# Attention in pairs of groups: one compressed softmax for eight heads, all transposes of a unit ahead of its value products

## The chip, the cores and the metric

The kernel runs on one core of a Trainium2 chip. What counts is the device time of one execution in microseconds (us); a kernel's time is the median of several executions. A core has TensorE (matrix products and transposes, results in PSUM banks), VectorE, ScalarE, GpSimd and SyncE, which issues transfers. Each engine runs its own instructions in a fixed order and waits on semaphores of the others.

## What is computed

Two decoder layers over 256 tokens of width 1024 in float32: gated linear attention first, native sparse attention (NSA) second. Only the second layer's attention is touched. It has 16 heads of width 64 in 4 groups of 4, and three branches. With 256 tokens, four blocks of 64 and sixteen selectable blocks every block is selected, so the selected branch is causal attention over all keys; the window of 512 covers all keys as well. The compressed branch attends to 15 blocks, of which a token sees those that have ended, and gives zero where there is none.

```python
s = jnp.einsum('bghtd,bgcd->bghtc', qb, kcmp)
valid = cmp_end[None, :] <= t[:, None]
pc = jax.nn.softmax(jnp.where(valid, s, NEG), axis=-1)
pc = jnp.where(jnp.any(valid, axis=-1)[:, None], pc, 0.0)
o_c = jnp.einsum('bghtc,bgcd->bghtd', pc, vcmp)
...
o_s = jnp.einsum('bghtks,bgtksd->bghtd', ps, v_sel)
...
o_w = jnp.einsum('bghts,bgsd->bghtd', jax.nn.softmax(s, axis=-1), vwin)
...
o = jnp.einsum('bshc,bshcd->bshd', gates, out).reshape(B, S, NSA_Q) * jax.nn.silu(z)
return o @ w_out.astype(jnp.float32)
```

## The kernel before

The tokens lie in two tiles of 128 (t = 0, 1). A *unit* is one group of four heads on one tile, `Unit(g, t)`: eight units. Products that need float32 accuracy are split into a high and a low part, so that one product becomes three (L211, L212, L213: high by high, high or low by the other); a weight is split by ScalarE (`hi`, L190) and by VectorE or GpSimd (`lo`, L196) from one of four buffers `raw` that transfers fill.

`scores()` of a unit runs per head: products of q with the high and low part of k (L1001; for t = 0 256 keys and 16 compressed ones in one bank, for t = 1 272 columns in one bank and 256 of the window branch in another that two heads share), VectorE's mask with the row's extreme (L1006), ScalarE's exponential with its sum (L1008), VectorE's addition of the compressed scores' mask into `cS` (L1027), and per two heads the coefficients gate/sum (L1039, L1041) by which GpSimd scales the probabilities P in place (L1045). After the fourth head `compressed()` (L1054 to L1060, with ScalarE's exponential L1056 between) makes the compressed probabilities of the four heads, 128 x 64.

`values()` of a unit has 2(t + 1) rounds, one for each branch and 128 keys. T of a round is four transposes of P into one bank (L1074) and a copy to pT, on ScalarE (L1078) and on VectorE (L1080) in turn; V of a round is two products of 64 columns of v with pT (L1088) that accumulate in half of the bank `o`, which the units use in turn. T runs two rounds ahead of V: T0, T1, V0, T2, V1, T3 and so on. In the last rounds but one stands Tc, the transpose of the compressed probabilities (L1094) with ScalarE's copy pcT (L1096), and the end is Vc, two products of pcT with the compressed values (L1112). `finish()` multiplies by the gate z and splits the result into `ofT` (L356 VectorE, L357 ScalarE, L358 VectorE).

Around them: `z_steps` (two projections for the gate, L211 to L213 of 256 columns, evacuated by L362), the loads and splits of the out-projection's weights, and `out_steps(t)`, 48 products of 512 columns per tile (L211 to L213 into two banks `acc`), of which an L213 is the first to need the low part of ofT. After the products of a bank the residual: L269 ScalarE, L271/L274/L276/L281 VectorE, L275 GpSimd, then the store.

The program text gives the units one after the other: units (0,0) and (1,0), z's first half, (2,0), z's second half, (3,0), `out_steps(0)`, then the four units of t = 1, and `out_steps(1)`. A scheduler of the framework sets the order of each engine's instructions from there, as its own estimate of the times decides; `after(ins, prev)` adds an edge that only fixes an order on the engine, `chain` ties the projections' products one behind the other, and one edge puts out_steps(1)'s products from k = 5 (`LATE`) behind the last product of unit (3,1). Banks of PSUM: acc 2, s (scores) 3, t (transposes) 2, o 1. Buffers: eight for P, three for pT.

Of the kernel before, what the change touches and what calls it, by code (L numbers as in the profile page):

```python
# [16 lines left out]
P = 128  # L17
# [70 lines left out]
def hybrid_kernel(ctx: ExitStack, tc: tile.TileContext, x, positions, pre_norm, post_norm,  # L88
# [893 lines left out]
    obank, on = bank("o"), [0]  # L982

    class Unit:


        def __init__(self, g, t):
            self.g, self.t, self.n = g, t, (t + 1) * P
            self.Pt = []

        def scores(self):
            g, t, n = self.g, self.t, self.n
            self.mn, self.sm, self.cS, self.cf = small(8, "mn"), small(8, "sm"), small(64, "cS"), small(8, "cf")
# [3 lines left out]
            c3 = self.cS.rearrange("p (h c) -> p h c", c=16)  # L997
# [12 lines left out]
            for i in range(4):  # L1010
# [244 lines left out]
```

## Time and profile before

| | us |
|---|---|
| three executions | 307.05, 307.33, 304.06; median 307.05 |
| the profiled execution | 302.72 |
| its span, first to last instruction | 300.8 |
| busy: TensorE / VectorE / ScalarE / GpSimd | 286.6 / 215.3 / 181.5 / 167.0 |
| mean granted TensorE clock | 0.984 of full speed |

Times within the span count from its first instruction; around it lie 1.9 us. The second layer's attention works from about 195 us to the end. A product's length in a timeline contains its filling of the pipeline, so that products that stand 0.23 us apart may each be 0.4 long: what a sequence costs is read from start to start. A line whose count is over one is several instructions in a row.

### The profile page before, as it was taken

Reading aid. Unit: us, or ns where it says so; the run is one execution under the profiler, and the core shown is the slowest. Engines: PE = TensorE matmul, PEld = TensorE weight load, DVE = VectorE, ACT = ScalarE, POOL = GpSimd, SP = SyncE. Lnnn points to the kernel's source line nnn. Section 1 sums busy time; section 2 is a strip of 40 time slices with the busy share of each in tenths; the row PEclk is TensorE's granted clock in tenths of the full one; section 3 lists DMA queues with packets and bytes.
Section 4 is the critical chain, followed back from the end, with each engine's and each line's share of the span. In section 5 each row is a group of like instructions: output and inputs, shape, how many; then the busy total and the mean of one; then the engine's idle time right before and its main releaser. Section 6 shows DMA issues by size and latency. Waiting matters only on the chain.

```text
span 300.8 us, 5374 instructions
## 1 busy us (share of the span) xinstructions
PE 286.6 (95%) x1788; PEld 239.7 (80%) x1788; DVE 215.3 (72%) x556; ACT 181.5 (60%) x468; POOL 167.0 (56%) x184
## 2 busy tenths in 40 slices
PE   7999999999999999889979999999997999999991
PEld 7888999999998887668958676899994678676660
DVE  1779569846979877576893536799999858877423
ACT  4896788667754757435534405679967637657301
POOL 1496968984383252927545035897799434172200
PEclk9999999999999999999999999999997799999998
DMA  7997588105677334394745785576144000100001
GB/s 214 403 362 217 151 258 288 56 22 186 204 220 212 92 82 130 64 289 147 195 162 144 274 263 180 190 218 232 42 142 139 2 0 0 71 2 0 2 0 71
DMA packets 28301, 44.57 MB, mean 148 GB/s; under 512 B 2865, under 2 KB 12513, under 8 KB 28274
## 3 DMA queue, kind: packets, MB, share of 16 engines
q1 hardware_dynamic: 28242, 44.23, 46.6%
q8 instruction: 14, 0.23, 0.3%
q14 instruction: 13, 0.11, 0.1%
q10 hardware_dynamic: 32, 0.01, 0.0%
HBM read 43.18 MB, written 1.05 MB: 147 GB/s over the span
## 4 chain that ended last, share of the span: by engine, by line
PE 63%; DVE 13%; issue 9%; POOL 6%; ACT 4%; DMA 3%; SPq 0%; POOLq 0%; DVEq 0%; ACTq 0%
PE acc L211 11%; PE acc L213 11%; PE acc L212 11%; PE s L468 4%; POOL lo L196 3%; PE s L212 3%; PE s L211 3%; PE s L213 3%; DVE lo L196 3%; PE o L894 3%; PE t L1074 3%; PE o L1088 3%; PE s L1001 2%; ACT hi L190 2%; DMA raw<-in_gla_w_in_dram 1%
## 5 line engine op out<-in xcount | busy, mean ns | idle before, releaser
L196 POOL TENSOR_TENSOR lo<-raw,hi 128x512 fp32r<-128x512 f32 (+2 forms) x63 | 82.8, 1334 | 44.4 <-ACT hi L190 44.4
L190 ACT ACTIVATE hi<-raw 128x512 fp32r<-128x512 f32 (+2 forms) x120 | 64.2, 583 | 37.7 <-DMA raw<-in_nsa_w_in_dram 26.6
L196 DVE TENSOR_TENSOR lo<-raw,hi 128x512 fp32r<-128x512 f32 (+2 forms) x57 | 53.6, 963 | 13.4 <-ACT hi L190 13.3
L1045 POOL TENSOR_SCALAR P<-P,cf 128x128 f32<-128x128 f32 (+1 forms) x64 | 29.2, 475 | 30.2 <-DVE cf L1041 14.4
L211 PE MATMUL acc<-hT,hi 128*128 128x256 f32 x160 | 45.2, 283 | 0.1
L212 PE MATMUL acc<-hT,hi 128*128 128x256 f32 x160 | 44.8, 280 | 0.0
L213 PE MATMUL acc<-hT,lo 128*128 128x256 f32 x160 | 44.5, 281 | 0.0
L211 PE MATMUL acc<-hi,hT 128*128 128x512 f32 (+2 forms) x112 | 39.2, 350 | 1.2 <-DVE yg L276 0.8
L213 PE MATMUL acc<-hi,hT 128*128 128x512 f32 (+2 forms) x112 | 38.9, 347 | 0.0
L212 PE MATMUL acc<-lo,hT 128*128 128x512 f32 (+2 forms) x112 | 38.8, 346 | 0.0
L1008 ACT ACTIVATE P<-P,mn 128x128 f32<-128x128 f32 (+1 forms) x64 | 28.4, 445 | 7.2 <-DVE mn L1006 5.9
L211 PEld LDWEIGHTS acc<-hT,hi 128*128 128x128 f32 x160 | 30.1, 188 | 0.4 <-DVE zT L362 0.3
L212 PEld LDWEIGHTS acc<-hT,hi 128*128 128x128 f32 x160 | 30.1, 188 | 0.1
L213 PEld LDWEIGHTS acc<-hT,lo 128*128 128x128 f32 x160 | 29.8, 188 | 0.0
L211 PEld LDWEIGHTS acc<-hi,hT 128*128 128x128 f32 x112 | 21.1, 188 | 5.3 <-ACT yg L269 1.2
L1006 DVE CUSTOM_DVE_ANT_0 P<-s,c 128x128 f32<-128x128 f32 (+1 forms) x64 | 20.6, 347 | 5.3 <-PE s L1001 4.4
L213 PEld LDWEIGHTS acc<-hi,hT 128*128 128x128 f32 x112 | 21.1, 188 | 2.9 <-DVE hT L311 0.4
L212 PEld LDWEIGHTS acc<-lo,hT 128*128 128x128 f32 x112 | 21.1, 188 | 2.0
L1074 PE MATMUL t<-c,P 128*128 128x128 f32 x96 | 17.4, 296 | 2.0 <-ACT pcT L1096 1.9
L440 POOL TENSOR_TENSOR lo<-raw,hi 128x512 fp32r<-128x512 f32 (+1 forms) x9 | 12.3, 1388 | 9.9 <-ACT hi L436 9.8
L1074 PEld LDWEIGHTS t<-c,P 128*128 128x128 f32 x96 | 11.1, 147 | 7.3 <-issue 3.6
L832 POOL TENSOR_TENSOR dup<-rt,rt 128x512 f32<-128x512 f32 x6 | 8.9, 1487 | 11.2 <-DVE rt L825 5.7
(268 smaller groups left out, 676.2 us busy)
## 6 DMA issues: line engine op xcount, KB each, us to landing
raw<-in_nsa_w_in_dram SPq DMA_DIRECT2D x24, 512.0 KB, 4.5
raw<-in_gla_w_in_dram SPq DMA_DIRECT2D x12, 512.0 KB, 6.1
raw<-in_gla_w_out_dram SPq DMA_DIRECT2D x8, 512.0 KB, 4.3
raw<-in_nsa_w_out_dram SPq DMA_DIRECT2D x8, 512.0 KB, 4.2
raw<-in_nsa_w_in_dram SPq DMA_DIRECT2D x8, 280.0 KB, 8.4
raw<-in_gla_w_in_dram SPq DMA_DIRECT2D x6, 344.0 KB, 3.4
home<-in_gla_w_in_dram SPq DMA_DIRECT2D x4, 512.0 KB, 6.7
w<-in_nsa_ck_w_dram SPq DMA_DIRECT2D x4, 512.0 KB, 3.8
```

The costliest lines, as they stand in the source:

```text
L190: m = after(nc.scalar.activation(hi[:, j, :n], raw[:, j, :n], AF.Copy), prev)
L196: eng.tensor_sub(lo[:, j, :n], raw[:, j, :n], f(hi[:, j, :n]))
L211: m = nc.tensor.matmul(o, a[0], b[0], start=start, stop=False, **kw)
L212: nc.tensor.matmul(o, a[0], b[1], start=False, stop=False, **kw)
L213: return m, nc.tensor.matmul(o, a[1], b[0], start=False, stop=stop, **kw)
L440: line(e, eng.tensor_sub(lo[:, j, :n], raw[:, j, :n], f(hi[:, j, :n])))
L468: m = nc.tensor.matmul(o[t][:, :chunk.n], hT[i][:, k, t * P:(t + 1) * P], w[j], start=(k == b == 0), stop=(k == KT - 1 and b == 2))
L894: nc.tensor.matmul(hid_b[kv * 64:(kv + 1) * 64, :CHID], flat[:, j, kv].rearrange("p g c -> p (g c)"), w1[u * 2 + kv][:, j % 4, :], start=( ...
L1006: nc.vector.tensor_tensor_reduce(out=o, in0=src, in1=masks[br], op0=ALU.add, op1=ALU.min, scale=-0.125, scalar=3.0e38, accum_out=self.mn[: ...
L1008: nc.scalar.activation(o, o, AF.Exp, scale=-1.0, bias=self.mn[:, j:j + 1], accum_out=self.sm[:, j:j + 1])
L1045: nc.gpsimd.tensor_scalar(o, o, cf[:, i * 2 + br:i * 2 + br + 1], 1.0, op0=ALU.mult, op1=ALU.mult)
L1074: pe(nc.tensor.transpose(b[:, i * P:(i + 1) * P], self.Pt[i][:, c0:c0 + P], ident))
```

## The change

A class `Pair` holds what two groups of a tile share: `cS` for eight heads (128 x 128), one compressed softmax for them (L1001 to L1007 in the changed file; the same seven operations as before, with 8 instead of 4 columns of sums), one bank with both transposes Tc (L1012) and one copy pcT (L1014), and Vc for either half (L1022). `scores()` is no generator any more; its lines are L1046 (products), L1051 (mask), L1053 (exponential), L1072 (cS), L1083/L1085 (coefficients) and L1089 (GpSimd). The text order is: scores of both groups, then values of both. `values()` issues all T of the unit (L1101; copies L1105 on ScalarE, L1108 on VectorE, the latter into two buffers of another pool, so that the three of pT are ScalarE's alone), in a pair's first unit then Tc, then all V (L1119), tied in their order and behind the last Vc before them, then Vc. The first V of a unit stands behind its last T or, in a pair's first unit, behind Tc. `out_steps(1)` gets two more edges: products from k = 1 behind T of the last unit's second round, from k = 2 behind T of its fourth. The bank `o` is shared as before; it is cleared only by the first product of a pair.

```diff
-    obank, on = bank("o"), [0]
+    obank, lastC = bank("o"), [None]
+
+    class Pair:
...
+        def begin(self):
+            self.cS = small(128, "cS")
+
+        def compressed(self):
+
+            p, t = self.p, self.t
+            gv = gates[:, t, 8 * p:8 * p + 8, :]
+            cS = self.cS
+            c3 = cS.rearrange("p (h c) -> p h c", c=16)
+            cm, cs = small(8, "cm"), small(8, "cs")
+            nc.vector.tensor_reduce(cm, c3, axis=AX.X, op=ALU.max)
+            nc.vector.tensor_tensor(c3, c3, cm.unsqueeze(2).to_broadcast([P, 8, 16]), op=ALU.subtract)
+            nc.scalar.activation(cS, cS, AF.Exp, scale=0.125)
+            nc.vector.tensor_reduce(cs, c3, axis=AX.X, op=ALU.add)
+            nc.vector.reciprocal(cs, cs)
+            nc.vector.scalar_tensor_tensor(cs, cs, cc("anyv")[:, t:t + 1], gv[:, :, 0], op0=ALU.mult, op1=ALU.mult)
+            nc.vector.tensor_tensor(c3, c3, cs.unsqueeze(2).to_broadcast([P, 8, 16]), op=ALU.mult)
+
+        def transpose(self):
+            b = bank()
+            for G in range(2):
+                self.Tc = nc.tensor.transpose(b[:64, G * P:(G + 1) * P], self.cS[:, G * 64:(G + 1) * 64], ident)
+            pcT = ap_.tile([64, 2 * P], F32, tag="pcT", name=nm("pcT"), bufs=1)
+            nc.scalar.activation(pcT, b[:64, :2 * P], AF.Copy)
+            self.pcT = pcT
+
+        def share(self, G, m):
+
+            ob = obank[:, G * 256:(G + 1) * 256]
+            for i in range(2):
+                w = vblk[:, 2 * self.p + G, 2 * i:2 * i + 2, :].rearrange("p a d -> p (a d)")
+                m = after(nc.tensor.matmul(ob[:, i * P:(i + 1) * P], w, self.pcT[:, G * P:(G + 1) * P], start=False,
+                                           stop=(i == 1), skip_group_check=True), m)
+            return m
 
...
         def scores(self):
             g, t, n = self.g, self.t, self.n
-            self.mn, self.sm, self.cS, self.cf = small(8, "mn"), small(8, "sm"), small(64, "cS"), small(8, "cf")
+            self.mn, self.sm, self.cf = small(8, "mn"), small(8, "sm"), small(8, "cf")
+            if g % 2 == 0:
+                self.pair.begin()
+            c3 = self.pair.cS[:, g % 2 * 64:(g % 2 + 1) * 64].rearrange("p (h c) -> p h c", c=16)
...
-                if i == 3:
-                    self.compressed()
-                yield 1
+            if g % 2:
+                self.pair.compressed()
...
         def values(self):
+
...
+            ob = obank[:, g % 2 * 256:(g % 2 + 1) * 256]
             rounds = [(br, y) for br in range(2) for y in range(t + 1)]
-            pTs = {}
...
+            pTs, self.T = [], []
+            for br, y in rounds:
                 b = bank()
                 c0 = br * n + y * P
                 for i in range(4):
-                    pe(nc.tensor.transpose(b[:, i * P:(i + 1) * P], self.Pt[i][:, c0:c0 + P], ident))
-                pT = ap_.tile([P, 512], F32, tag="pT", name=nm("pT"), bufs=N_PT)
+                    m = nc.tensor.transpose(b[:, i * P:(i + 1) * P], self.Pt[i][:, c0:c0 + P], ident)
                 evac[0] += 1
                 if evac[0] % 2:
+                    pT = ap_.tile([P, 512], F32, tag="pT", name=nm("pT"), bufs=N_PT)
                     nc.scalar.activation(pT, b, AF.Copy)
                 else:
+                    pT = lp.tile([P, 512], F32, tag="rt1", name=nm("pT"), bufs=2)
                     nc.vector.tensor_copy(pT, b)
-                pTs[r] = pT
-
...
+                pTs.append(pT)
+                self.T.append(m)
+            if g % 2 == 0:
+                self.pair.transpose()
+                m = self.pair.Tc
+
+            for r, (br, y) in enumerate(rounds):
                 kt = (t - y) if br == 0 else y
                 pv = pTs[r].rearrange("p (i a n) -> p a i n", i=2, a=2)
                 for a in range(2):
-                    pe(nc.tensor.matmul(ob[a * 64:(a + 1) * 64, :],
-                                        (vs_sb, vw_sb)[br][:, kt, g * DH:(g + 1) * DH], pv[:, a],
-                                        start=(br == y == 0), stop=False, skip_group_check=True))
-
...
+                    v = nc.tensor.matmul(ob[a * 64:(a + 1) * 64, :], (vs_sb, vw_sb)[br][:, kt, g * DH:(g + 1) * DH],
+                                         pv[:, a], start=(r == 0 and g % 2 == 0), stop=False, skip_group_check=True)
+                    if r == 0:
+                        after(after(v, m), lastC[0])
+                    else:
+                        after(v, self.lastV)
+                    self.lastV = v
+            self.last = lastC[0] = self.pair.share(g % 2, self.lastV)
...
         for k, n in steps:
             a, b = mm3(o[n], [h[:, k, :] for h in ofT[t]], ch_o[n].part(k), k == 0, k == KT - 1)
-            if before and (k, n) == (LATE, 0):
-                after(a, before())
+            if n == 0 and k in before:
+                after(a, before[k])
             chain(a, b)
...
-    unit(0, 0)
+    U[0, 0].scores()
+    U[1, 0].scores()
+    U[0, 0].values()
     q_T(1, 1)
-    unit(1, 0)
+    U[1, 0].values()
...
-    unit(2, 0)
+    U[2, 0].scores()
+    U[3, 0].scores()
+    U[2, 0].values()
     ch_z[1].load().split((ch_z[0], PA[11]))
     run(z_steps(1))
-    unit(3, 0)
+    U[3, 0].values()
...
-    for g in range(GROUPS):
-        unit(g, 1)
-        U[g, 1].finish()
-    run(out_steps(1, lambda: U[3, 1].last))
+    for p in range(2):
+        for g in range(2):
+            U[2 * p + g, 1].scores()
+        for g in range(2):
+            U[2 * p + g, 1].values()
+            U[2 * p + g, 1].finish()
+    u = U[3, 1]
+    run(out_steps(1, {1: u.T[1], 2: u.T[3], LATE: u.last}))
```

The order that the scheduler makes of it, at three places. First TensorE behind z's second half (names: s scores, t transposes, o value products, acc projections; q of the second tile is qS_2221 here). Before, unit (1,0) with its first round of value products, its Tc and the first transposes of unit (2,0) behind it:

```order
L1074 MATMUL t_2457<-c_64,P_2395 128x128 x2
L1074 MATMUL t_2457<-c_64,P_2418 128x128 x2
L1088 MATMUL o_2022<-pT_2455,vs_sb 64x256 x2
L1094 MATMUL t_2466<-c_64,cS_2393 64x128
L1074 MATMUL t_2679<-c_64,P_2624 128x128 x2
L1074 MATMUL t_2679<-c_64,P_2647 128x128 x2
L1088 MATMUL o_2022<-pT_2462,vw_sb 64x256 x2
L1112 MATMUL o_2022<-pcT_2468,vblk 128x128 x2
```

And now, from unit (0,0)'s Vc behind z's second half on:

```order
L1022 MATMUL o_2022<-pcT_2423,vblk 128x128 x2
L1101 MATMUL t_2441<-c_64,P_2351 128x128 x2
L1101 MATMUL t_2441<-c_64,P_2374 128x128 x2
L1046 MATMUL s_3068<-kTh,qS_2221 128x272
L1046 MATMUL s_3068<-kTl,qS_2221 128x272
L1046 MATMUL s_3044<-kTh,qS_2221 128x256
L1046 MATMUL s_3044<-kTl,qS_2221 128x256
L1046 MATMUL s_3073<-kTh,qS_2221 128x256
L1046 MATMUL s_3073<-kTl,qS_2221 128x256
L1101 MATMUL t_2448<-c_64,P_2351 128x128 x2
L1101 MATMUL t_2448<-c_64,P_2374 128x128 x2
L1119 MATMUL o_2022<-pT_2446,vs_sb 64x256 x2
```

Before, the transpose of unit (1,0)'s compressed probabilities (L1094) stood there between its value products and unit (2,0)'s transposes; now the first pair's Tc stands ahead of z's end, and unit (0,1)'s scores (256 and 272 columns) stand around unit (1,0)'s transposes and value products.

Second, VectorE up to the second L358 of the first pair of groups, behind which out_steps(0) can use the low part of ofT (ISA with P is the mask). Before:

```order
L1006 ISA P_2868,mn_2841<-s_2877,c_65 128x128
L1006 ISA mn_2841 128x1
L1006 ISA P_2868,mn_2841<-s_2877,c_65 128x128
L1006 ISA mn_2841 128x1
L1027 TENSOR_TENSOR cS_2843<-s_2877,c_65 128x16
L1006 ISA P_3064,mn_3060<-s_3065,c_65 128x256
L1006 ISA mn_3060 128x1
L1006 ISA P_3064,mn_3060<-s_3070,c_65 128x256
L1006 ISA mn_3060 128x1
L358 TENSOR_TENSOR ofT_2213<-of_2612,ofT_2212 128x256
L358 TENSOR_TENSOR ofT_2213<-of_2616,ofT_2212 128x256
```

Now:

```order
L1108 COPY pT_2727<-t_2722 128x512
L1051 ISA P_3099,mn_3096<-s_3105,c_65 128x256
L1051 ISA mn_3096 128x1
L1051 ISA P_3111,mn_3096<-s_3112,c_65 128x256
L1051 ISA mn_3096 128x1
L1072 TENSOR_TENSOR cS_3037<-s_3112,c_65 128x16
L1083 RECIPROCAL cf_3036<-sm_3035 128x4
L1085 TENSOR_TENSOR cf_3036<-cf_3036,gates 128x4
L358 TENSOR_TENSOR ofT_2213<-of_2599,ofT_2212 128x256
L358 TENSOR_TENSOR ofT_2213<-of_2603,ofT_2212 128x256
```

Before, two masks of the second tile (256 columns) stood ahead of L358; now eleven do, of which these rows show the last three, and the masks of unit (3,0) (128 columns) stand ahead of z's gating instead of here.

Third, TensorE at the last pair's transposes of compressed probabilities. Before, in unit (2,1):

```order
L1088 MATMUL o_2022<-pT_3386,vw_sb 64x256 x2
L1094 MATMUL t_3399<-c_64,cS_3296 64x128
L1088 MATMUL o_2022<-pT_3395,vw_sb 64x256 x2
L1074 MATMUL t_3482<-c_64,P_3415 128x128
L1074 MATMUL t_3482<-c_64,P_3427 128x128
L1074 MATMUL t_3482<-c_64,P_3444 128x128
L1074 MATMUL t_3482<-c_64,P_3456 128x128
L1112 MATMUL o_2022<-pcT_3401,vblk 128x128 x2
```

Now:

```order
L1101 MATMUL t_3408<-c_64,P_3288 128x128
L1101 MATMUL t_3408<-c_64,P_3300 128x128
L1046 MATMUL s_3355<-kTh,qS_2436 128x256
L1046 MATMUL s_3355<-kTl,qS_2436 128x256
L1012 MATMUL t_3415<-c_64,cS_3258 64x128 x2
L1119 MATMUL o_2022<-pT_3392,vs_sb 64x256 x2
L1119 MATMUL o_2022<-pT_3399,vs_sb 64x256 x2
L1119 MATMUL o_2022<-pT_3406,vw_sb 64x256 x2
L1119 MATMUL o_2022<-pT_3413,vw_sb 64x256 x2
L1101 MATMUL t_3434<-c_64,P_3320 128x128
L1101 MATMUL t_3434<-c_64,P_3332 128x128
L1101 MATMUL t_3434<-c_64,P_3349 128x128
```

Before, L1094 stood between value products with out-projection products ahead of them; now L1012, for both groups, stands directly behind the last score products of unit (3,1) and in front of all value products of unit (2,1). VectorE's rows there are now:

```order
L1108 COPY pT_3413<-t_3408 128x512
L1001 TENSOR_REDUCE cm_3378<-cS_3258 128x8
L1051 ISA P_3361,mn_3317<-s_3355,c_65 128x256
L1051 ISA mn_3317 128x1
L1002 TENSOR_TENSOR cS_3258<-cS_3258,cm_3378 128x128
L1083 RECIPROCAL cf_3319<-sm_3318 128x4
L1085 TENSOR_TENSOR cf_3319<-cf_3319,gates 128x4
L1004 TENSOR_REDUCE cs_3379<-cS_3258 128x8
L1005 RECIPROCAL cs_3379<-cs_3379 128x8
L1006 SCALAR_TENSOR_TENSOR cs_3379<-cs_3379,c_65,gates 128x8
L1007 TENSOR_TENSOR cS_3258<-cS_3258,cs_3379 128x128
```

The softmax of eight heads begins behind the copy of unit (2,1)'s last transposes (pT_3413) and has the mask of those last scores (P_3361) and two coefficient operations between its own.

## Rows read from the trace of the kernel before

**Rows 1.** The page: busy time of TensorE in us with its share of the span and its instructions, and from the span in 40 equal slices (7.5 us each) the busy share of TensorE and its granted clock, in tenths.
```profile
PE 286.6 (95%) x1788; PEld 239.7 (80%) x1788; DVE 215.3 (72%) x556; ACT 181.5 (60%) x468; POOL 167.0 (56%) x184
...
PE   7999999999999999889979999999997999999991
...
PEclk9999999999999999999999999999997799999998
```

**Rows 2.** Busy time of each engine in stretches of the span (in brackets the instructions that begin there; behind the engines the granted clock of TensorE as a share of full speed, the share of the DMA engines and GB/s).
```profile
215.00:225.00 10.00, 10.00 (x81) 8.71 (x80) 9.87 (x29) 7.50 (x22) 9.88 (x11) 1.00 0.31 107
225.00:235.00 10.00, 8.12 (x43) 5.88 (x42) 9.91 (x30) 6.68 (x22) 8.42 (x10) 0.73 0.31 107
...
265.00:285.00 20.00, 20.00 (x128) 13.50 (x126) 12.93 (x57) 10.79 (x36) 7.89 (x17) 1.00 0.00 1
...
228.00:230.00 2.00, 0.21 (x1) 0.05 (x2) 2.00 (x13) 1.86 (x7) 2.00 (x4) 0.92 0.64 239
230.00:236.00 6.00, 6.00 (x24) 4.36 (x26) 6.00 (x15) 3.92 (x13) 3.42 (x3) 0.50 0.00 1
236.00:238.00 2.00, 2.00 (x12) 0.63 (x8) 2.00 (x13) 0.98 (x6) 1.85 (x4) 0.87 0.00 0
```

**Rows 3.** The timeline of all engines at the end: start and length in us, engine, line, operation, tiles, shapes, count. The last product and the last store's issue.
```profile
294.14 0.40 PE L213 MATMUL acc<-hi,ofT 128*128 128x512 f32 x1
...
296.90 0.99 SPq L125 DMA_DIRECT2D out_dram<-x_sb  x2
```

**Rows 4.** TensorE's timeline where z's projection ends; in brackets idle time in front and what ended it.
```profile
225.63 0.28 PE L213 MATMUL acc<-hT,lo 128*128 128x256 f32 x1
225.74 0.29 PE L1001 MATMUL s<-kTh,qS 128*128 128x272 f32 x1
225.87 0.29 PE L1001 MATMUL s<-kTl,qS 128*128 128x272 f32 x1
...
227.92 0.30 PE L1094 MATMUL t<-c,cS 128*64 128x128 f32 x1
230.00 1.09 PE L1074 MATMUL t<-c,P 128*128 128x128 f32 x4 [1.79 <-ACT pcT L1096]
```

**Rows 5.** TensorE's timeline at another gap, in the compression of keys.
```profile
151.26 0.65 PE L894 MATMUL o<-w,flat 128*64 128x256 f32 x2
153.48 0.87 PE L894 MATMUL o<-w,flat 128*64 128x256 f32 x6 [1.57 <-DVE flat L885]
```

**Rows 6.** Instructions from 195 us to the end, grouped by line, operation and shape: busy us, mean ns of one, idle time in front.
```profile
L1006 DVE CUSTOM_DVE_ANT_0 P<-s,c 128x256 f32<-128x256 f32 x32 | 12.8, 415 | 5.2 <-PE s L1001 4.4 <-PE t L1074 0.7
...
L196 DVE TENSOR_TENSOR lo<-raw,hi 128x512 fp32r<-128x512 f32 x9 | 9.1, 1020 | 0.1
...
L1006 DVE CUSTOM_DVE_ANT_0 P<-s,c 128x128 f32<-128x128 f32 x32 | 7.8, 279 | 0.1
...
L1060 DVE TENSOR_TENSOR cS<-cS,cs 128x64 f32<-128x64 f32 x8 | 4.6, 576 | 0.1
...
L1055 DVE TENSOR_TENSOR cS<-cS,cm 128x64 f32<-128x64 f32 x8 | 3.1, 391 | 0.1
```

**Rows 7.** VectorE's timeline in the stretch that the change works on, from the gating of z (L362) to the second subtraction of ofT (L358, two instructions).
```profile
226.97 0.69 DVE L362 TENSOR_TENSOR zT<-acc,rb 128x512 f32<-128x512 f32 x1
...
230.95 1.32 DVE L1060 TENSOR_TENSOR cS<-cS,cs 128x64 f32<-128x64 f32 x1
...
236.73 0.41 DVE L1006 CUSTOM_DVE_ANT_0 P<-s,c 128x256 f32<-128x256 f32 x1
...
237.08 0.75 DVE L358 TENSOR_TENSOR ofT<-of,ofT 128x256 fp32r<-128x256 f32 x2
```

**Rows 8.** VectorE's timeline around one unit's compressed softmax in the second tile, and behind it two rows of ScalarE's timeline for the same time.
```profile
266.46 0.68 DVE L1080 COPY pT<-t 128x512 f32<-128x512 f32 x1
267.06 0.20 DVE L1054 TENSOR_REDUCE cm<-cS 128x4 f32<-128x64 f32 x1
...
269.81 0.48 DVE L1060 TENSOR_TENSOR cS<-cS,cs 128x64 f32<-128x64 f32 x1
...
268.14 0.58 ACT L1078 ACTIVATE pT<-t 128x512 f32<-128x512 f32 x1
268.62 0.25 ACT L1056 ACTIVATE cS<-cS 128x64 f32<-128x64 f32 x1
```

**Rows 9.** TensorE's timeline at the first L213 product of out_steps(0) (the first that reads the low part of ofT).
```profile
239.54 0.48 PE L213 MATMUL acc<-hi,ofT 128*128 128x512 f32 x1
...
240.54 0.39 PE L211 MATMUL acc<-hi,ofT 128*128 128x512 f32 x1
240.77 0.40 PE L212 MATMUL acc<-lo,ofT 128*128 128x512 f32 x1
```

**Rows 10.** TensorE's timeline in the second tile.
```profile
258.93 0.66 PE L1074 MATMUL t<-c,P 128*128 128x128 f32 x4
259.51 0.65 PE L1088 MATMUL o<-pT,vs_sb 128*64 128x256 f32 x4
260.10 0.66 PE L1074 MATMUL t<-c,P 128*128 128x128 f32 x4
260.51 0.37 PE L1001 MATMUL s<-kTh,qS 128*128 128x272 f32 x1
...
262.26 0.41 PE L1074 MATMUL t<-c,P 128*128 128x128 f32 x2 [0.16 <-ACT pcT L1096]
```

More of the change, by code (lines that the diff above doesn't have):

```diff
@@ L996, in scores @@
             masks = (C2[:, o:o + n], C2[:, o + 3 * P - n:o + 3 * P])
-            c3 = self.cS.rearrange("p (h c) -> p h c", c=16)
             def mm(o, i, c0, c1):
@@ L1087, in V @@
                 for a in range(2):
-                    pe(nc.tensor.matmul(ob[a * 64:(a + 1) * 64, :],
-                                        (vs_sb, vw_sb)[br][:, kt, g * DH:(g + 1) * DH], pv[:, a],
-                                        start=(br == y == 0), stop=False, skip_group_check=True))
-            def Tc():
-                b = bank()
-                pe(nc.tensor.transpose(b[:64, :P], self.cS, ident))
-                pcT = ap_.tile([64, P], F32, tag="pcT", name=nm("pcT"), bufs=2)
-                nc.scalar.activation(pcT, b[:64, :P], AF.Copy)
-                self.pcT = pcT
-            T(0)
-            yield 1
-            T(1)
-            yield 1
-            R = len(rounds)
-            for r in range(R):
-                V(r)
-                if r + 2 < R:
-                    T(r + 2)
-                elif r + 2 == R:
-                    Tc()
-                yield 1
-            for i in range(2):
-                self.last = pe(nc.tensor.matmul(ob[:, i * P:(i + 1) * P], vblk[:, g, 2 * i:2 * i + 2, :].rearrange("p a d -> p (a d)"),
-                                    self.pcT, start=False, stop=(i == 1), skip_group_check=True))
-            yield 1
+                    v = nc.tensor.matmul(ob[a * 64:(a + 1) * 64, :], (vs_sb, vw_sb)[br][:, kt, g * DH:(g + 1) * DH],
[6 more added lines that the diff above has]
+            self.last = lastC[0] = self.pair.share(g % 2, self.lastV)
         def finish(self):
@@ L1118, in finish, with out_steps @@
             sl = slice(2 * g, 2 * g + 2)
-            gated(self.ob.rearrange("p (i n) -> p i n", i=2), zT[:, sl, t * P:(t + 1) * P],
-                  *(a[:, sl, :] for a in ofT[t]))
-    def slot(unit, nxt, fill, nfill):
-        val, sc = unit.values(), nxt.scores() if nxt else iter(())
-        nv = 4 + 2 * unit.t + 1
-        for i in range(nv):
-            run(val, 1)
-            run(sc, 1)
-            run(fill, (i + 1) * nfill // nv - i * nfill // nv)
-        run(sc)
-    def out_steps(t, before=None):
+            gated(obank[:, g % 2 * 256:(g % 2 + 1) * 256].rearrange("p (i n) -> p i n", i=2),
+                  zT[:, sl, t * P:(t + 1) * P], *(a[:, sl, :] for a in ofT[t]))
+    def out_steps(t, before={}):
         o = [bank("acc") for _ in range(2)]
@@ L1193, in hybrid_kernel @@
     ch_o = [Chunk(nsa_w_out[0], c * 512, 512) for c in range(2)]
+    pairs = {(p, t): Pair(p, t) for p in range(2) for t in range(NT)}
     U = {(g, t): Unit(g, t) for g in range(GROUPS) for t in range(NT)}
-    def unit(g, t):
-        run(U[g, t].scores())
-        run(U[g, t].values())
     q_T(0, 1)
```

23 lines of the change are left out of this document (4 added, 19 removed).

## The prediction

> **What bounds the kernel now.** I read the page's busy times first: TensorE is busy for 95% of the span, so at most 14 us can be won in all, and the slices of its busy share and of its granted clock [rows 1] say that the only place after the start where both drop is around three quarters of the span, just where the change works. Then the table by stretches [rows 2]: from 215 to 225 us TensorE and VectorE are both full (10.00 and 9.87 of 10); from 225 to 235 VectorE stays full (9.91) while TensorE has 8.12 at a granted clock of 0.73; from 265 to 285 TensorE is full at 1.00 and VectorE has 12.93 of 20. So the end of the kernel has two stages. Up to about 237 us VectorE sets the pace. Behind that TensorE does, to its last product at 294.14 us, and 6.3 us of residual and store follow [rows 3], which the change leaves as they are.
>
> TensorE's own timeline shows the seam [rows 4]: z's last product starts at 225.63, a transpose of the compressed probabilities (L1094) runs at 227.92, and the next transposes come only at 230.00, 1.79 us of it idle behind ScalarE's copy L1096. Between 228 and 230 TensorE is busy 0.21 us; from 230 to 236 the granted clock is 0.50, and behind it 0.87 on the mean of two more us [rows 2]. That is the lower of the two levels, 1.2 instead of 2.4 GHz, and about 6.5 us of products ran at it. Another gap, from 151.26 to 153.48 with 1.57 us idle [rows 5], lies in slices whose granted clock shows no fall [rows 1]: a gap of some 2 us may cost the clock or not.
>
> **The change part by part.**
>
> *One compressed softmax for eight heads.* The two elementwise lines of VectorE in it (L1055, L1060) cost 7.7 us over eight units [rows 6]. After it there are four of each, 64 elements wider. Going from 128 to 256 columns the mask operation goes from 279 to 415 ns, so 64 more are worth some 0.07 us: 3.9 + 4 x 2 x 0.07 = 4.4 us, 3.3 us less on VectorE (with the four small operations, which only halve, somewhat more); half of it lies before 240 us, where VectorE binds. Some of these operations are long because of their neighbours: L1060 takes 1.32 us at 230.95 [rows 7], in a stretch where GpSimd is full too [rows 2], against 0.48 us at 269.81 [rows 8].
>
> *The order of the first stretch.* Both units' scores of a pair now come before either's value products, so unit (3,0)'s scores stand before z's end, and eleven of the second tile's masks (256 wide) stand on VectorE ahead of the second ofT subtraction L358, for which the first L213 product of out_steps(0) waits. Before, the stretch on VectorE from the first L362 (226.97) to the end of that L358 (237.83) takes 10.9 us [rows 7]. After, I count in it from the order: 11 masks at 0.35 us from start to start, 3 splits L196 at 0.7 to 1.0, 2 of L969 and 2 copies (512 columns each) at 0.6 from start to start, 2 of L362 at 0.6, four operations of the compressed softmax (1.7), L356 and L358 twice (1.5), coefficients and additions (1.2) [rows 6 to 8]: 3.8 + 2.5 + 2.4 + 1.2 + 1.7 + 1.5 + 1.2 = 14.3 us. That sum begins at about 227 us, since the added scores ahead of it (eight masks of 0.25 us and their additions, about 2.5 us) and the merged softmax (about 2.5 us less there) balance. So L358 ends near 241.3 us, and the L213 product that started at 239.54 [rows 9] starts about **2.0 us later**. Lower bound: 1.0 us earlier than before, if the stretched operations (1.32 for 0.48 us, and splits of 1.02 for 0.7) shrink to what they take alone; upper: 4.5 us later, with every split at its 1.02 us and a wait of half a mask behind the products in front of each of the eleven.
>
> *What has been done by then.* At that product the new order has 20 score products, 5 transposes and one transpose of compressed probabilities more behind it than the old one at its own. Score products stand 0.13 us apart [rows 4] and four transposes take 0.41 us [rows 10]: 20 x 0.125 + 5 x 0.1 + 0.1 = **3.1 us less** to do afterwards. Since TensorE sets the pace there, this counts in full.
>
> *All transposes, then all value products.* A round of value products (two, which the trace shows as four instructions of 256 columns) takes 0.58 us in front of transposes, and four transposes in front of a round 0.58, while four transposes in front of scores take 0.41 [rows 10]. Four times 256 columns at the pace of the 512-column out-projection (0.23 us) [rows 9] would be 0.46. A switch to value products and back thus costs at most 0.17 + 0.12 = 0.29 us, and I take 0.24, since the first part stands in a row and of the second I count half. Counted in the order, 10 of the 18 runs of value products (with those of the compressed branch) in the second tile are left; only the first unit of each pair has its four rounds in one: 8 x 0.24 = **1.9 us less** (0 to 2.3). The Trainium skill, TensorE: Matmul & The Clock Gate, Part 2 (step-by-step), says that weight loads are pulled ahead of products in flight, by which the switch would be free, this term 0 and the time 1.9 us higher. The rows disagree: the same four transposes cost 0.41 or 0.58 us by what follows.
>
> *The wait that the grouping makes.* Each pair's transposes of compressed probabilities (L1012) now stand in front of the first unit's value products. For the last pair the last score products of unit (3,1) stand directly ahead of it, and nothing else: TensorE must stand still from there until the softmax of eight heads is done, because all value products are queued behind L1012 and everything else behind them. Before, products of out_steps and value products lay there and waits of this kind cost 0.16 us [rows 10]. The chain on VectorE is the same sequence as at 267.06 to 270.29 us (maximum, a mask, subtraction, coefficients, sum, reciprocal, two products), 3.23 us [rows 8]. I take off 0.48 for ScalarE's copy at 268.14, which the new order puts elsewhere, and add 4 x 0.07 for the width: 3.0. In front of it VectorE copies the pT of the last transposes, 0.6 us, of which TensorE's last two score products hide about 0.2. So the gap is **3.4 us** (2.7 without the copy and the width, 4.2 with ScalarE late as well).
>
> *The rest.* Waits like the 0.16 us at 262.26 [rows 10] go and others of the same kind (scores behind the two heads that share a bank) come: 0, by estimate from -0.9 to +0.9 (some six of them). The edges in out_steps(1) only spread 48 products that TensorE must run anyway. VectorE's copies of pT go to other buffers at the same length: 0, behind TensorE.
>
> Sum: +2.0 - 3.1 - 1.9 + 3.4 = +0.4 us on the profiled execution's 302.7, so 303.1. That execution is the fastest of four (304.06, 307.05, 307.33 besides; mean 305.3), 2.6 us below their mean. A median should read about 303.1 + 2.6 = **305.7 us**. A measurement here tells about 1% (3 us) from no change.
>
> **The rivals.** *A: the sum as it stands.* 305.7; with each term at moderate distance 303 to 308.
>
> *B: the clock falls in the new gap.* In 2.09 us without transposes at 228 us it fell, and 6.5 us of products ran at half [rows 2, 4], which loses 3.2 us. For: the new gap is longer, and short products with waits surround it. Against: TensorE is full at 1.00 from 265 to 285 [rows 2], where the new gap comes. Own time 303.1 + 3.2 = 306.3, **308.9 us**, slower by a little more than 1%. The rows show one gap in which the clock fell and one in which it didn't, so I give this about one in four. The Trainium skill, same page, Why this matters for your kernels, says that idle gaps between bursts bring the clock back to its low level; by it alone this case would be the likelier.
>
> *C: the relief of VectorE is worth more.* If L358 ends so that the L213 product comes at 238.5 (-1.0), the gap is 2.7 and the switches give 2.3: -1.0 - 3.1 - 2.3 + 2.7 = -3.7, own 299.0, **301.6 us**, faster. For: VectorE is full exactly there, and L1060 was stretched nearly threefold. Against: a split and nine wide masks more than before stand in that stretch, for eight narrow ones less.
>
> *D: the first stretch is slowed by the clock.* By the paces above some 9.5 us of TensorE work lie in the new stretch from 228 to 241.3. If the clock falls at 229.7 as before and stays at half, 1.7 + 11.6/2 = 7.5 us of it are done at 241.3, and the rest takes 2 us at full or 4 at half: TensorE binds in VectorE's place, and the L213 product comes at about 244 (+4.5). +4.5 - 3.1 - 1.9 + 3.4 = +2.9, own 305.6, **308.2 us**. A start after 241.1 makes the kernel slower at all, one after 244 by 1%. Against it: the gap at 227.92 goes, as other units' work stands there.
>
> *E: grouping saves nothing.* If a round of value products takes 0.58 us for its own sake (64-column weights) and transposes in front of it wait for its operands rather than for the switch, the term is 0: own 305.0, **307.6 us**.
>
> **How the numbers follow.** A 0.37, C 0.27, B 0.22, D 0.09, E 0.05. The range goes from C with a fast set of executions, 300.3, to B with a term at its bound, 310.0; it leaves out about 2 in 10. Faster by over 1%: C's and a little of A, 0.31. Slower by over 1%: most of B, half of D, some of A, 0.29. Within: 0.40. A's own range is 303 to 308.
>
> **What would show it.** Right: the first L213 product of out_steps(0) at 240.5 to 242.5; one idle stretch of TensorE of about 3.4 us that ends with L1012 some 17 us before the end of products; value products L1119 standing 0.46 us apart per round within a run; last product 6.3 us before the end of the span. Wrong: a granted clock of 0.5 behind that gap (B), L213 before 239.5 (C), a half clock through 230 to 241 (D), rounds of L1119 still 0.58 apart (E).

## The result and the profile after

The changed kernel takes 307.6 us (median of 19 executions, 305.35 to 308.97), the kernel before 303.94 beside it (19, 302.02 to 307.45): 1.0123 times as long, 95% interval 1.0106 to 1.0139. The change costs 3.7 us; no change worth measuring was forecast. The profiled execution took 307.21 us, its span 305.2, 4.4 more than that of before. Some executions of a kernel are disturbed (longer, at a lower granted clock); the ratios here leave these out, the medians of e5, e6 and e8 in the table below do not, and e6, whose profile is of one, has no parts there.

The page: busy time of the engines, and TensorE's busy share and granted clock in slices of 7.6 us, as [rows 1].

```profile
PE 285.3 (93%) x1788; PEld 240.8 (79%) x1788; DVE 211.9 (69%) x532; ACT 180.0 (59%) x460; POOL 167.4 (55%) x184
...
PE   7999999999999999989989999999996999995991
...
PEclk9999999999999999999999999999999799996897
```

There are two dips of the clock before the end instead of one. The stretches, as [rows 2]:

```profile
225.00:235.00 10.00, 6.90 (x48) 5.24 (x48) 9.87 (x31) 9.90 (x29) 10.00 (x13) 1.00 0.35 107
235.00:245.00 10.00, 9.82 (x56) 6.83 (x53) 9.73 (x34) 6.80 (x20) 5.65 (x10) 0.83 0.01 2
...
265.00:275.00 10.00, 9.43 (x66) 6.73 (x64) 6.94 (x31) 6.07 (x20) 4.16 (x9) 1.00 0.00 1
275.00:285.00 10.00, 6.83 (x31) 4.12 (x32) 2.85 (x12) 2.18 (x8) 1.88 (x4) 0.66 0.01 2
...
276.00:278.00 2.00, 0.00 (x0) 0.00 (x0) 1.45 (x6) 0.58 (x3) 1.05 (x3) 0.80 0.00 0
278.00:280.00 2.00, 1.83 (x8) 0.95 (x10) 0.03 (x1) 0.38 (x1) 0.83 (x2) 0.50 0.00 0
...
282.00:284.00 2.00, 2.00 (x9) 1.35 (x8) 0.00 (x0) 0.46 (x1) 0.00 (x0) 0.50 0.03 8
284.00:286.00 2.00, 2.00 (x13) 1.66 (x13) 1.42 (x3) 0.55 (x2) 0.00 (x0) 0.99 0.00 0
```

From 225 to 235 us TensorE has 6.90 instead of 8.12, VectorE is as full as before; from 275 to 285 it has 6.83 where it was full before, and from 278 to 284 the granted clock is 0.50, the lower of the two levels. TensorE's timeline from z's last product to the first L213 of out_steps(0), as [rows 4, 9]:

```profile
226.00 0.28 PE L213 MATMUL acc<-hT,lo 128*128 128x256 f32 x1
...
228.86 0.37 PE L1046 MATMUL s<-kTh,qS 128*128 128x272 f32 x1 [0.62 <-DVE cS L1072]
...
230.47 0.36 PE L1046 MATMUL s<-kTh,qS 128*128 128x256 f32 x1 [0.85 <-DVE cf L1083]
...
234.04 0.39 PE L1046 MATMUL s<-kTh,qS 128*128 128x256 f32 x1 [1.63 <-DVE mn L1051]
...
243.78 0.39 PE L213 MATMUL acc<-hi,ofT 128*128 128x512 f32 x1
```

The 1.79 us of before are gone, but three waits on VectorE, 3.1 us, stand in their place, and L213 comes 17.8 us behind z's last product instead of 13.9. VectorE in the same time, as [rows 7], and a row of GpSimd's timeline:

```profile
226.25 1.27 DVE L362 TENSOR_TENSOR zT<-acc,rb 128x512 f32<-128x512 f32 x2
...
230.83 1.23 DVE L1085 TENSOR_TENSOR cf<-cf,gates 128x4 f32<-128x4 f32 x1
...
232.21 1.09 DVE L1006 SCALAR_TENSOR_TENSOR cs<-cs,c,gates 128x8 f32<-128x8 f32 x1
...
234.59 1.30 DVE L1007 TENSOR_TENSOR cS<-cS,cs 128x128 f32<-128x128 f32 x1
...
241.28 0.76 DVE L358 TENSOR_TENSOR ofT<-of,ofT 128x256 fp32r<-128x256 f32 x2
```

```profile
229.54 6.20 POOL L196 TENSOR_TENSOR lo<-raw,hi 128x512 fp32r<-128x512 f32 x5
```

From the first L362 (226.25) to the end of L358 (242.04) it takes 15.8 us. Three operations on few columns take 1.1 to 1.3 us each while GpSimd splits weights for 6.2 us. And L213 does not start with L358's end but 1.7 us behind it, as before (239.54 against 237.83), because TensorE has other rows in front. Then the last pair's Tc, TensorE and behind it VectorE, as [rows 8, 10]:

```profile
274.44 0.28 PE L1046 MATMUL s<-kTl,qS 128*128 128x256 f32 x1
278.17 0.61 PE L1012 MATMUL t<-c,cS 128*64 128x128 f32 x2 [3.45 <-DVE cS L1007]
278.71 1.98 PE L1119 MATMUL o<-pT,vs_sb 128*64 128x256 f32 x8
280.47 1.92 PE L1119 MATMUL o<-pT,vw_sb 128*64 128x256 f32 x8
282.32 1.12 PE L1101 MATMUL t<-c,P 128*128 128x128 f32 x4
```

```profile
274.52 0.69 DVE L1108 COPY pT<-t 128x512 f32<-128x512 f32 x1
275.13 0.28 DVE L1001 TENSOR_REDUCE cm<-cS 128x8 f32<-128x128 f32 x1
...
277.52 0.51 DVE L1007 TENSOR_TENSOR cS<-cS,cs 128x128 f32<-128x128 f32 x1
```

TensorE stands still for 3.45 us. Behind that, eight instructions of value products (two rounds) take 1.76 us from start to start, twice 0.88. The last product, as [rows 3]:

```profile
298.63 0.39 PE L213 MATMUL acc<-hi,ofT 128*128 128x512 f32 x1
```

It stands 4.49 us later than before; what follows is as long as before.

### The profile page after: what moved, and what is told of

It is laid out like the page before. It is cut to its first block, busy times and chain, and to the rows that moved or that the text cites. A ratio compares the mean times of both kernels' runs of the same rounds, so it can differ in the third digit from the quotient of the medians.

```text
span 305.2 us, 5335 instructions
## 1 busy us (share of the span) xinstructions
PE 285.3 (93%) x1788; PEld 240.8 (79%) x1788; DVE 211.9 (69%) x532; ACT 180.0 (59%) x460; POOL 167.4 (55%) x184
## 4 chain that ended last, share of the span: by engine, by line
PE 60%; DVE 16%; issue 12%; ACT 4%; POOL 4%; DMA 2%; SPq 0%; POOLq 0%; DVEq 0%; ACTq 0%
PE acc L211 11%; PE acc L213 10%; PE acc L212 10%; PE s L468 4%; PE s L212 3%; PE s L211 3%; PE s L213 3%; DVE lo L196 3%; PE o L894 3%; PE t L1101 3%; DVE P L1051 2%; PE o L1119 2%; PE s L1046 2%; ACT hi L190 2%; DMA raw<-in_gla_w_in_dram 2%
## 5 line engine op out<-in xcount | busy, mean ns | idle before, releaser
L196 DVE TENSOR_TENSOR lo<-raw,hi 128x512 fp32r<-128x512 f32 (+2 forms) x57 | 52.7, 947 | 12.8 <-ACT hi L190 12.6
L213 PE MATMUL acc<-hT,lo 128*128 128x256 f32 x160 | 44.4, 281 | 0.0
L1089 POOL TENSOR_SCALAR P<-P,cf 128x128 f32<-128x128 f32 (+1 forms) x64 | 30.0, 488 | 25.3 <-ACT P L1053 12.3
L213 PE MATMUL acc<-hi,hT 128*128 128x512 f32 (+2 forms) x112 | 38.9, 348 | 0.0
L1053 ACT ACTIVATE P<-P,mn 128x128 f32<-128x128 f32 (+1 forms) x64 | 28.4, 445 | 14.9 <-DVE mn L1051 11.6
L213 PEld LDWEIGHTS acc<-hT,lo 128*128 128x128 f32 x160 | 29.8, 188 | 0.0
L1051 DVE CUSTOM_DVE_ANT_0 P<-s,c 128x128 f32<-128x128 f32 (+1 forms) x64 | 20.5, 347 | 7.2 <-PE s L1046 6.7
L213 PEld LDWEIGHTS acc<-hi,hT 128*128 128x128 f32 x112 | 21.0, 188 | 2.9 <-DVE hT L311 0.4
L1046 PE MATMUL s<-kTh,qS 128*128 128x272 f32 (+1 forms) x48 | 14.9, 326 | 3.1 <-DVE mn L1051 1.6
L275 POOL TENSOR_TENSOR ss<-ss,cols 128x1 f32<-128x1 f32 x4 | 2.2, 554 | 27.7 <-DVE ss L274 27.7
L1101 PE MATMUL t<-c,P 128*128 128x128 f32 x96 | 16.3, 295 | 0.7 <-DVE pT L1108 0.3
```

The costliest lines, as they stand in the source:

```text
L196: eng.tensor_sub(lo[:, j, :n], raw[:, j, :n], f(hi[:, j, :n]))
L213: return m, nc.tensor.matmul(o, a[1], b[0], start=False, stop=stop, **kw)
L1046: pe(nc.tensor.matmul(o, q[i], k[:, g, c0:c1], start=(m == 0), stop=(m == 1)))
L1051: nc.vector.tensor_tensor_reduce(out=o, in0=src, in1=masks[br], op0=ALU.add, op1=ALU.min, scale=-0.125, scalar=3.0e38, accum_out=self.mn[: ...
L1053: nc.scalar.activation(o, o, AF.Exp, scale=-1.0, bias=self.mn[:, j:j + 1], accum_out=self.sm[:, j:j + 1])
L1089: nc.gpsimd.tensor_scalar(o, o, cf[:, i * 2 + br:i * 2 + br + 1], 1.0, op0=ALU.mult, op1=ALU.mult)
```

## The experiments

Two theories. G: the loss is the wait at the last pair's Tc, which costs its 3.45 us and then the clock. F: the loss is the longer first stretch. Each run is timed beside the kernel before, whose medians were 303.4 to 303.9 us, and the ratios are to it. The two parts of the time are read from TensorE's timelines: from the start of z's last product to the first L213 of out_steps(0), and from there to the start of the last product.

| kernel | ratio (interval) | median us | to out_steps(0), us | from there, us |
|---|---|---|---|---|
| before | | 303.9 | 13.9 | 54.6 |
| changed | 1.0123 (1.0106 to 1.0139) | 307.6 | 17.8 | 54.9 |
| e1 gap filled | 1.0041 (1.0008 to 1.0073) | 305.1 | 17.7 | 52.1 |
| e2 no edges | 0.9940 (0.9911 to 0.9968) | 301.6 | 19.0 | 49.0 |
| e3 pairs, first tile | 1.0004 (0.9975 to 1.0033) | 303.9 | 18.8 | 51.3 |
| e4 pairs, second tile | 1.0112 (1.0078 to 1.0146) | 307.1 | 14.3 | 58.1 |
| e5 Tc late | 1.0068 (1.0038 to 1.0098) | 306.3 | 21.0 | 50.4 |
| e6 Tc late, no edges | 0.9951 (0.9913 to 0.9989) | 303.5 | | |
| e7 second tile, no edges | 0.9993 (0.9958 to 1.0027) | 303.1 | 14.4 | 53.6 |
| e8 grouping alone | 0.9988 (0.9962 to 1.0014) | 303.5 | 15.5 | 54.9 |
| e9 Tc late, second tile | 1.0008 (0.9981 to 1.0035) | 304.3 | 17.7 | 51.1 |
| e10 the same, no edges | 0.9947 (0.9922 to 0.9971) | 302.0 | 17.7 | 49.7 |
| e11 masks behind | 1.0121 (1.0077 to 1.0166) | 307.6 | 15.3 | 57.5 |

The parts are those of one profiled execution of each kernel, the ratios from many: the profiled execution of before is 1.2 us under its median, that of e2 3.2 us above.

**e1: the wait stays, the clock is kept.**

```diff
+            if (self.p, self.t) == (1, 1):
+                m = lastS[0]
+                for i in range(FILL):
+                    m = after(nc.tensor.transpose(b[:, 256 + i % 2 * P:256 + (i % 2 + 1) * P], ident, ident), m)
             for G in range(2):
                 self.Tc = nc.tensor.transpose(b[:64, G * P:(G + 1) * P], self.cS[:, G * 64:(G + 1) * 64], ident)
```

(`lastS` is the last score product; one more edge keeps unit (3,1)'s first transposes where they were; `FILL` is 28.)

> The changed kernel with 28 transposes of a constant, whose results nobody reads, in the idle time ahead of the last pair's Tc; every other row of TensorE's order is as in the changed kernel. Theory G (the wait at the last Tc costs twice: 3.45 us idle and then the half clock): the gap stays filled to about 0.5 us, the granted clock stays at 1.00 there, the products behind it run at full speed, so 2.9 us less than the changed kernel's 307.6: 304.7. Theory F (the loss comes from the first stretch, where out_steps(0) starts 4.2 us later, and the clock falls for other reasons than the idle time): 307.6 as before the edit, or the clock falls all the same.

TensorE's timeline, and two stretches:

```profile
274.20 0.28 PE L1051 MATMUL s<-kTl,qS 128*128 128x256 f32 x1
274.61 3.27 PE L1015 MATMUL t<-c 128*128 128x128 f32 x28
277.93 0.38 PE L1017 MATMUL t<-c,cS 128*64 128x128 f32 x2
278.24 1.08 PE L1126 MATMUL o<-pT,vs_sb 128*64 128x256 f32 x8
279.15 1.03 PE L1126 MATMUL o<-pT,vw_sb 128*64 128x256 f32 x8
280.12 0.66 PE L1106 MATMUL t<-c,P 128*128 128x128 f32 x4
```

```profile
235.00:245.00 10.00, 8.73 (x57) 6.09 (x54) 9.81 (x34) 7.04 (x21) 5.64 (x11) 1.00 0.01 2
275.00:285.00 10.00, 9.95 (x79) 7.64 (x77) 4.32 (x14) 2.83 (x8) 1.87 (x4) 1.00 0.01 2
```

Tc starts 3.73 us behind the start of the last score product, as in the changed kernel (274.44 to 278.17), but the clock stays at 1.00 and two rounds take 0.91 us from start to start. The ratio falls from 1.0123 to 1.0041, 2.5 us (1.4 to 3.6, an estimate from the two intervals): that is the clock's share of the loss, and F fails here. It is not a matter of the profiled executions alone: the mean granted clock, as the median of all executions, goes from 0.976 to 0.987. What is left is 1.2 us (0.2 to 2.2).

**e2: real products in the wait.**

```diff
-    run(out_steps(1, {1: u.T[1], 2: u.T[3], LATE: u.last}))
+    run(out_steps(1, {LATE: u.last}))
```

> The changed kernel without the two new edges that hold products of out_steps(1) behind the last unit's transposes; in the order ten of them then stand ahead of the last Tc. Theory G: the gap shrinks by 10 x 0.23 = 2.3 us and the clock does not fall, 2.3 + 2.9 less than 307.6: 302.4. Theory F: the products that fill the gap are missed later, where the edges let them cover the last unit's waits: 2 to 3 us of it are given back, 305 to 307.

The last product ahead of Tc, Tc, and the stretch behind:

```profile
281.47 0.40 PE L213 MATMUL acc<-hi,ofT 128*128 128x512 f32 x1
282.83 0.38 PE L1012 MATMUL t<-c,cS 128*64 128x128 f32 x2 [0.96 <-DVE cS L1007]
```

```profile
285.00:295.00 10.00, 10.00 (x60) 7.08 (x59) 2.99 (x6) 2.03 (x4) 0.00 (x0) 1.00 0.00 0
```

0.96 us of the wait are left, the clock does not fall behind it, and the kernel is 0.6% faster than the kernel before: against the changed kernel 5.6 us (1.0123 to 0.9940) from two edges. Nothing of it is given back later: 49.0 us from out_steps(0) on. The 19.0 us ahead of it are another matter. The profiled execution is the slowest of e2's twelve (304.83), z's last product comes 2.2 us later in it than in the changed kernel (228.19 against 226.00), and behind that, with the changed kernel's order of instructions, the clock fell:

```profile
235.00:245.00 10.00, 8.79 (x39) 5.89 (x39) 9.41 (x33) 7.78 (x25) 5.64 (x10) 0.66 0.01 2
```

e10, with the same rows there at 1.00, takes 17.7.

**e3 and e4: one tile at a time.** The other tile's units are the kernel before's class and text order (e4 has `PAIRED = (1,)`; e3 has no new edges in out_steps(1), e4 has both).

```diff
+PAIRED = (0,)
-    U = {(g, t): Unit(g, t) for g in range(GROUPS) for t in range(NT)}
+    U = {(g, t): (Unit if t in PAIRED else UnitB)(g, t) for g in range(GROUPS) for t in range(NT)}
```

> Pairs for the first tile only; the second tile's four units as before the change (one after the other, T two rounds ahead of V, own softmax). Theory G: the first stretch is longer by 4.2 us but 3.1 us of later work is done in it, so some 1 us over the kernel before: 305.0. Theory F: all of the loss is there, 307 to 308.

> Pairs for the second tile only; the first tile's units in the text order and form of before, and TensorE's order is that of before up to out_steps(0). Theory G: the gap and the half clock stay (3.45 + 2.9) and the grouping's gain too (1.9 and 0.9 of small waits): about 2.7 us over the kernel before, 306.5. Theory F: as before the change or better, 301 to 304.

The loss is in the second tile: 1.0004 against 1.0112. e3 takes 18.8 us to out_steps(0), 4.9 more, and 51.3 behind it, 3.3 less: the longer first stretch is for the most part paid for by the work done in it. Of the 1.6 us that the profiles leave, 1.4 are the distance of the two profiled executions from their medians; by the ratio the first tile costs 0.1 us (-0.8 to +1.0). e4's wait, TensorE's timeline:

```profile
279.35 0.61 PE L1013 MATMUL t<-c,cS 128*64 128x128 f32 x2 [3.44 <-DVE cS L1008]
```

**e5: Tc behind the value products.**

```diff
-            if g % 2 == 0:
-                self.pair.transpose()
-                m = self.pair.Tc
...
+            if g % 2 == 0:
+                self.pair.transpose()
             self.last = lastC[0] = self.pair.share(g % 2, self.lastV)
```

> The changed kernel with a pair's Tc, and its copy pcT, behind the first unit's value products instead of in front of them; the two edges stay. Theory G: the four rounds of the last pair (1.9 us at 0.47 each) go into the wait, which shrinks to about 1.5 us, too short for the clock: 1.9 + 2.5 less than 307.6: 303.2. Theory F: the wait only moves behind the value products, with the same total and the same fall of the clock: 307.

The expected time was missed: 1.0068 is 1.7 us under the changed kernel, not 4.4. TensorE's timeline at the last pair, and two stretches:

```profile
278.64 1.03 PE L1115 MATMUL o<-pT,vw_sb 128*64 128x256 f32 x8
281.31 0.38 PE L1012 MATMUL t<-c,cS 128*64 128x128 f32 x2 [1.64 <-DVE cS L1007]
```

```profile
235.00:245.00 10.00, 8.48 (x39) 5.72 (x38) 7.56 (x31) 5.76 (x19) 4.77 (x11) 0.61 0.01 2
...
275.00:285.00 10.00, 7.90 (x58) 5.97 (x57) 7.28 (x28) 5.23 (x16) 3.71 (x8) 1.00 0.01 2
```

Where it was expected, it came: 1.64 us of wait, no half clock behind it, and 50.4 us from out_steps(0) on, 4.4 less than the changed kernel. But the edit moved the first tile's Tc too, and there the granted clock is 0.61 from 235 to 245: 21.0 us instead of 17.8. That this is why the time was missed is tested by e9.

**e6, e7, e8.** (e6: the edits of e2 and e5 together. e7: e4 without the two edges.)

> Both edits: Tc behind the first unit's value products, and no new edges in out_steps(1). Theory G: e2 left 0.96 us of wait at the last Tc; it goes as well, so e2's 301.6 less 0.9: 300.7. Rival: the products that e2 put into the wait now stand in front of value products that could have run, and nothing is won over e2: 301.6.

> Pairs for the second tile only, first tile as before, without the two edges. Theory G: pairs for the first tile are worth nothing (e3: 1.0004), so this is e2 again, 301.6; if the two halves help each other it is nearer the kernel before, 303.4.

> The kernel before, with one part of the change alone: in the second tile's units all four T ahead of all four V, tied in their order, and VectorE's pT in two buffers of the other pool; softmax, Tc and everything else as before, unit by unit. The price of 0.11 us for a round of V and 0.17 for T in front of it, with four switches fewer in the order than before: 1.0 us under the kernel before, 302.4. Rival: V waits for four copies instead of one, and the later V hold back finish() and the next unit: as before or above, 303.4 to 305.

e6 is e2 again (0.9951 and 0.9940): filling the same wait twice wins nothing more. e7 is not e2 again but near the kernel before, as its second case said: without the edges, pairs for the first tile are worth 0.5% (e2 against e7, intervals that just overlap), with them nothing (changed against e4); the runs don't tell why. e8 (edit: `T(2)` and `T(3)` ahead of the loop over V, V tied to the last T and to each other, and VectorE's pT in two buffers of the other pool) is inconclusive: its interval has room for the expected gain of 1 us (0.9967) and for none.

**e9 and e10: e5's edit for the second tile alone** (`g % 2 == 0 and t == 0` keeps the first tile's Tc in front).

> e5 for the second tile only: there Tc behind the first unit's value products, in the first tile in front of them as in the changed kernel; the two edges stay. In e5's trace out_steps(0) to the last product took 50.4 us instead of the changed kernel's 54.9, but z's end to out_steps(0) 21.0 instead of 17.8 at a half clock. Theory G: the second number of e5 without the first, 4.4 us under 307.6: 303.2. Rival: e5's whole effect again, 305.7.

> e9 without the two edges. Theory G: the last wait goes and e2's first stretch stays: e2's 301.6 less its remaining 0.96 us: 300.7. Rival: filling the wait twice wins nothing over e2: 301.6 or more.

e9's wait, and two stretches:

```profile
278.86 0.38 PE L1012 MATMUL t<-c,cS 128*64 128x128 f32 x2 [1.30 <-DVE cS L1007]
```

```profile
235.00:245.00 10.00, 8.73 (x57) 6.09 (x54) 9.81 (x34) 7.03 (x21) 5.64 (x11) 1.00 0.01 2
275.00:285.00 10.00, 8.67 (x62) 6.15 (x60) 5.50 (x17) 3.85 (x12) 3.70 (x8) 1.00 0.01 2
```

1.30 us of wait, 51.1 us from out_steps(0) on; the ratio 1.0008 lies 3.5 us under the changed kernel's, 4.4 were expected. e10 is e2 within the intervals (302.0, where 300.7 was expected), so the two ways of filling the wait are the same gain once.

**e11: VectorE's queue in the first stretch**, on top of e2.

```diff
+                if (g, t) == (0, 1) and i > 0:
+                    after(m, U[1, 0].fin)
```

(`m` is the mask, `fin` the second L358.)

> e2 with one more edge on VectorE: the second tile's masks from the second head of unit (0,1) on stand behind the second L358 of the first pair, as before the change; in the order two masks of 256 columns stand ahead of it, not eleven. Theory Q (VectorE's queue ahead of L358 is what makes the first stretch longer): the nine masks with their additions, 3.5 us, leave it, so out_steps(0)'s first L213 comes 14 to 15 us behind z's last product instead of 19.0, TensorE has products for the masks' time, and some 2 us of its waits go: 299.6. Rival W (work is only moved: what is not done ahead of out_steps(0) comes behind it, and the waits with it): 301.6.

TensorE's timeline at four places, and a stretch:

```profile
234.29 0.65 PE L1121 MATMUL o<-pT,vw_sb 128*64 128x256 f32 x4 [2.55 <-DVE pT L1110]
...
241.51 0.48 PE L213 MATMUL acc<-hi,ofT 128*128 128x512 f32 x1
...
259.46 1.13 PE L1103 MATMUL t<-c,P 128*128 128x128 f32 x8 [0.53 <-ACT pT L1107]
...
262.48 0.39 PE L1046 MATMUL s<-kTh,qS 128*128 128x256 f32 x1 [1.65 <-DVE mn L1051]
```

```profile
265.00:275.00 10.00, 10.00 (x61) 6.63 (x59) 4.88 (x25) 4.84 (x15) 5.40 (x12) 0.77 0.01 2
```

L213 comes at 241.51, 15.3 us behind z's last product, near what Q says. But neither Q's time came (299.6) nor W's (301.6): at 1.0121 all of e2's gain is lost, 5.5 us. A wait of 2.55 us on VectorE's pT stands in the first stretch. Behind it VectorE is late: the eleventh mask of the second tile, at 251.75, comes 25.5 us behind z's last product instead of 14.7 in e2, and the first pair's softmax begins here:

```profile
259.00 0.28 DVE L1001 TENSOR_REDUCE cm<-cS 128x8 f32<-128x128 f32 x1
```

In e2 it begins at 254.08. TensorE waits at 259 for ScalarE's copy (0.53) and at 262 for the tile's eighteenth mask (1.65; a pair has sixteen), and behind that the clock falls: 0.77 from 265 to 275. What the masks brought along, then, is a later VectorE where TensorE binds; how much of the 5.5 us is these waits and how much the clock, no run shows.

## Why the prediction was wrong, point by point

- **The wait that the grouping makes**: its size was right (3.4 forecast, 3.45 measured, 3.44 in e4). The failed step is that the sum took it without the clock. The fall of the clock was rival B, with 0.22 and 3.2 us. It fell, in the changed kernel's profile for some 6.8 us (0.8 us of it in 276 to 278, all of 278 to 284), of which 5.9 had products to run: 2.9 us by the trace, 2.5 by e1. In e4's profile it fell there too, for about half as long. B's price was right, its chance too low: what was held against it, that TensorE is full at 1.00 ahead of the gap, did not protect it (from 265 to 275 the changed kernel has 9.43 of 10 at 1.00). The gap in which the clock had not fallen was 1.57 us long, not 3.4. With the clock kept, in e1, 1.2 us (0.2 to 2.2) are left, and the sum's +0.4 lies within that.
- **The order of the first stretch** was mis-sized: +2.0 forecast, +4.2 measured (239.54 to 243.78), within the bounds. 1.5 of it is an error in the sum: L358's new end was set against L213's old start, which lies 1.7 us behind L358 in both kernels. The rest is 15.8 instead of 14.3 us on VectorE, whose sum began 0.7 us earlier than assumed: three operations near 1.2 us where GpSimd splits. One L1085 takes 1.23, where the count had 1.2 for all coefficients and additions, and the four of the softmax take 2.8, where it had 1.7.
- **What has been done by then**: 3.1 forecast, about 4.1 measured. The numbers were right: behind out_steps(0) TensorE has 56 score products and 69 transposes before, 36 and 64 now. But the 20 score products were priced at 0.125 us, as they follow one another. Taken from start to start, score products cost 9.4 us there before and 5.8 in e1 (the changed order at full clock): 3.6 us less, 0.18 each, as other rows stand between them. With this term and the one before, the first tile is worth nothing, which e3's ratio says too; the forecast had it at -1.1.
- **All T, then all V**: within a run rounds stand 0.47 us apart (e1: 278.24 to 280.12, four rounds), 0.46 forecast, 0.58 before. Right for the round, and nearly for the term: behind out_steps(0) value products and transposes together take 18.3 us from start to start before and 16.1 in e1, of which the five transposes fewer are 0.5; that leaves 1.7, where 1.9 was forecast. That a kernel gains this from the grouping alone is not shown: e8's interval has room for both.
- **The rest**: 0 forecast, 0 measured. Behind out_steps(0), without the wait at Tc, TensorE waits 0.32 us in all before and 0.30 in the changed kernel.
- **The base**: the forecast added 2.6 us to the profiled execution, from four executions. The median of before, timed beside the changed kernel, is 303.94, only 1.2 above that execution. With 1.2 the sum would have read 304.3 and B 307.5, so 305.7 stood nearer to the measured 307.6 than its terms did, by luck.

Together, with the clock at 2.5 to 2.9: 0.4 + 2.2 - 1.0 + 0.2 + 2.5 to 2.9 = 4.3 to 4.7, against 4.49 at the last product. C is refuted by L213 at 243.78 and E by the rounds; E's 307.6 is the measured median by chance. Rival D's mechanism is seen in e5 and in e2's profiled execution (the clock in the first stretch), not in the changed kernel, where the fall from 236 to 240 costs little: e1, without it, takes 17.7 us there instead of 17.8.

## What to carry to other kernels

A product that waits for a long chain on other engines should not stand in front of a block that could run; where it must, look in the order at what lies between its last input and it, and put independent products there. A wait of TensorE is to be priced with what may follow it: here 3.45 us of wait brought a half clock that cost 2.5 to 2.9 us more, and two edges that held ten products back cost 5.6 us. And a stretch that is lengthened by moving work into it is to be read with the stretch that gets shorter: e3's first part alone reads as a loss of 4.9 us, and its ratio shows none.

## What the hardware showed unexpectedly

The same order of instructions runs at different clocks in different executions. In the first stretch the changed kernel, e1, e2 and e9 have the same rows on TensorE, and their profiled executions show 0.83, 1.00, 0.66 and 1.00 from 235 to 245 us. Executions of one kernel lie 4 us apart and more here (e2: 300.55 to 304.83), and one profile does not say which clock a stretch gets. The Trainium skill, TensorE: Matmul & The Clock Gate, Why this matters for your kernels, says that idle gaps between bursts bring the clock back to its low level: the gap at Tc agrees (1.00, 3.45 us idle, then 0.50), e9's gap of 1.30 us shows no fall. The length of a gap alone does not tell: a fall followed 1.79 us idle in the kernel before, and none followed 1.64 us at e5's last Tc.
